# Two-layer decoder trunk on one core: the order of the MLP's loads, products and norms is changed

## The chip, the cores and the metric

The kernel runs on one core of one Trainium2 chip. The metric is the device time of one execution in microseconds (us), lower is better. One core has five engines with a queue each (TensorE = PE, VectorE = DVE, ScalarE = ACT, GpSimd = POOL, SyncE = SP); all DMAs of this kernel that matter here are issued by SP, in the order of its queue.

## The reference, cut to what matters

A trunk of one layer A (stick-breaking attention) and one layer B (differential attention), width 1024, 1024 tokens and 16 meta tokens, each layer with the same MLP (hidden width 4096):

```python
def rmsnorm(x, g):
    y = xf * lax.rsqrt(jnp.mean(xf * xf, axis=-1, keepdims=True) + EPS)
    return y * g
def squared_relu_mlp(x, g, w_in, w_out):
    h = rmsnorm(x, g)
    return jnp.square(jax.nn.relu(h @ w_in)) @ w_out
...
x = x + attention(...); x = x + squared_relu_mlp(x, ...)   # A, then B
```

## The kernel before, in words

Every float32 factor is held as a high and a low part (`acopy` casts the high part on ACT, `tt` subtracts to the low part on DVE); a product is three matmuls (high·high, high·low, low·high). `mlp_stage` (line 736) does one layer's MLP, with names ending in `a` for layer A and in `b` for layer B. Both matrix products of the MLP are done by a seven-product scheme for 2x2 blocks: sums and differences of blocks are formed on DVE, and seven block products take the place of eight. The order of instructions on each engine is made by a scheduler that may move an instruction ahead of others which it doesn't depend on; `pin` and `keep_in_program_order` hold an instruction at its place in the program.

- **Transition** (`step`, L768 on). The attention's output projection is summed into `opa` (one tile for 128 output features and one chunk of tokens, 24 matmuls) and added to the residual `hs`; squares are gathered in `acca`. After tile 3 of the next chunk `rms_of` sums the squares by `rsa` matmuls, after tile 4 `normed` spreads the factor by `rba` transposes and DVE scales `h` (L117). Before these steps `w_split` prepares the seven weight operands of unit 0 (`w1a` to `w7a`).
- **Units** (`unit`, L919). There are 16 units, each making 256 hidden features by seven products `mia`. Unit 0 runs in two parts, for the two halves of the tokens; its product order is `PROD0` = 1, 2, 5, 3, 6, 7, 4 (L732), that of the others `PROD1` = 1, 5, 6, 2, 7, 3, 4. During unit 0's first part the norm of the second half is made (`second`, L1009), and the seven operands of that half (`ops7`: `xca`, `y3a`, `y6a`, `y7a`, `xda`) are cast and subtracted. At its end each unit stores seven results to DRAM (`u_d`, L979).
- **Out-products** (loop L1083). The seven products of `PROD2` = 2, 1, 6, 7, 4, 5, 3 follow, each of 16 steps `fi`. A step loads `ba` (L1091, from `u_d`) and in products 2 and 3, for every second step, `a12a` (L1095): this is the streamed part. Other weights stay resident: `r11a` (four loads), `ra0a`, `ra1a` (three each) and `ra2a` (two), 1 MB each, L1062, and the residual `hqa` (L1058, eight loads of 0.5 MB). The table `loads` (L1063) places them among the steps, but nothing pins them. `wba`, `waa` are the split operands in eight buffers, `moa` the sums in PSUM (24 matmuls of 260 columns a step in A; `mob`, 12 of 512 columns in B).
- **End of the stage.** After the last product (3) `half_add` adds all of `moa` to `hqa`, `row` in `epilogue_a` casts to the next stage's input `xb` and gathers squares in `accx`, and `norms` sums them (`rsx`). Layer B starts with the weights of head 0: `bws` (L1308, three loads each) scaled on POOL (L1314), split into `bwh`, `bwl`, used by `bpj`; `xm`, the meta tokens, is copied on POOL by `pcopy` (L124). In B the stage ends with stores to the output (L1570).

Of the kernel before, what the change touches and what calls it, by code (L numbers as in the profile page):

```python
# [17 lines left out]
P = 128  # L18
# [60 lines left out]
def kernel(ctx: ExitStack, tc: tile.TileContext, inp, out):  # L79
# [652 lines left out]
    PROD0, PROD1 = (1, 2, 5, 3, 6, 7, 4), (1, 5, 6, 2, 7, 3, 4)  # L732
# [3 lines left out]
    def mlp_stage(li, WO, wo_src, wo_scale, O, views, kf, gcol, base, close_w, chunk_done, epilogue):  # L736
# [122 lines left out]
        def ops7(c):  # L859

            h = hs[c]
            B11, B12, B21, B22 = (h[:, 4 * kh:4 * kh + 4, nh * nn:nh * nn + nn] for kh in range(2) for nh in range(2))

            return [lambda: put(c, 1, B11), lambda: put(c, 2, B21), lambda: tt(B11, B12, B11, ALU.subtract),
                    lambda: put(c, 5, B11), lambda: put(c, 3, B22), lambda: tt(B12, B22, B12, ALU.subtract),
                    lambda: tt(B22, B22, B11, ALU.subtract), lambda: put(c, 6, B22), lambda: put(c, 7, B12),
                    lambda: tt(B21, B21, B22, ALU.subtract), lambda: put(c, 4, B21)]
# [51 lines left out]
        def unit(u, parts, prods, more):  # L919
# [6 lines left out]
            for pi, cs in enumerate(parts):  # L926
# [12 lines left out]
                for pn, i in enumerate(prods):  # L939
# [49 lines left out]
        for i in PROD1:  # L989
            w_split(0, i)  # L990

        for ci, v in enumerate(order):
            for m in range(NMF, KT):
                step(m, v, 0)
                if ci and m == NMF:
                    chunk_done(hs, order[ci - 1], ps1, srow)
                    r = rms_of(order[ci - 1])
                if ci and m == NMF + 1:
                    normed(order[ci - 1], r)
                    if ci == 2:  # L1000
# [11 lines left out]
        def second(pi, pn):  # L1012
# [6 lines left out]
            elif pn == 2:  # L1019
# [3 lines left out]
                X7[0] = {1: xc[:, 0], 2: xc[:, 1], 5: xc[:, 2]} | {i: xblk(f"y{i}{tag}") for i in (3, 6, 7)}  # L1023
# [5 lines left out]
        unit(0, ((1,), (0,)), PROD0, second)  # L1029
        st_h0.close()  # L1030
        for u in range(1, NPAIR):
            unit(u, ((0, 1),), PROD1, lambda *a: None)
# [16 lines left out]
        def load_q(mh, nh):  # L1049

            for h in range(2):
                if li:
                    o = 512 * h + 256 * nh
                    nc.sync.dma_start(out=H[:, 4 * h + 2 * nh:4 * h + 2 * nh + 2, 512 * mh:512 * mh + 512],
                                      in_=y_d[o:o + 256, 512 * mh:512 * mh + 512].rearrange("(b q) n -> q b n", q=P))
# [8 lines left out]
        loads = {2: {1: [lambda: load_w(-1, 0)], 4: [lambda: load_w(-1, 4)], 7: [lambda: load_w(-1, 8)],  # L1064
                     9: [lambda: load_q(0, 0)], 11: [lambda: load_w(-1, 12)], 14: [lambda: load_w(0, 0), lambda: load_w(1, 0)]},
# [4 lines left out]
        def half_add(mh, nh, pss):  # L1070

            for x, ps in enumerate(pss):
                if li:
                    hv = H[:, 4 * (x // 2) + 2 * nh + x % 2, 512 * mh:512 * mh + 512]
                else:
                    m, h = divmod(x, 2)
                    hv = H[:, 4 * mh + m, half * h + nn * nh:half * h + nn * nh + nn]
                tt(hv, hv, ps, ALU.add)

        pss = None  # L1080
        for i in PROD2:
            if i in (2, 1, 5):
                qs = [ps2(f"mo{tag}_{i}_{x}") for x in range(2 if li else 4)]  # L1083
                pss = [q[:, x, :512 if li else nn] for q in qs for x in range(2)]
            a12 = None
            for fi in range(NPAIR):
                for fn in loads.get(i, {}).get(fi, ()):
                    fn()
                a11, a21, a22 = r11[:, fi], res(0, fi)[:, 0], res(1, fi)[:, 0]
                bs = srow(f"b{tag}_{i}_{fi}")[:, :half]  # L1090
                nc.sync.dma_start(out=bs, in_=u_d[:, fi, i - 1, :half])  # L1091
                if i in (2, 3):
                    if fi % 2 == 0:
                        a12 = raw(f"a12{tag}_{i}_{fi}").rearrange("p a b -> p (a b)").rearrange("p (f n) -> p f n", n=512)
                        nc.sync.dma_start(out=a12, in_=wr[1, :, fi:fi + 2, :512])  # L1095
                    a = a12[:, fi % 2]
                    if i == 3:
                        tt(a, a, a11, ALU.subtract)
                elif i == 7:
                    a = srow(f"a{tag}_{i}_{fi}")[:, :512]  # L1100
                    tt(a, a22, a11, ALU.subtract)
                else:
                    if i == 6:
                        tt(a21, a21, a22, ALU.add)
                        tt(a11, a21, a11, ALU.subtract)
                    a = {1: a11, 6: a11, 4: a22, 5: a21}[i]
                w, b = wop(f"wa{tag}_{i}_{fi}"), wop(f"wb{tag}_{i}_{fi}")
                for t, s, n in ((w, a, 512), (b, bs, half)):
                    acopy(t[:, 0, :n], s)
                    tt(t[:, 1, :n], s, f(t[:, 0, :n]), ALU.subtract)  # L1110
                first, last = fi == 0 and i in (2, 1, 5), fi == NPAIR - 1
                for x, ps in enumerate(pss):
                    for wi, (p, q) in enumerate(((0, 0), (0, 1), (1, 0))):
                        if li:
                            mm(ps, b[:, p, x * P:x * P + P], w[:, q, :512], first and wi == 0, last and wi == 2, skip_group_check=True)
                        else:
                            m, h = divmod(x, 2)
                            mm(ps, w[:, p, m * P:m * P + P], b[:, q, h * nn:h * nn + nn], first and wi == 0, last and wi == 2,
                               skip_group_check=True)
                work(3)  # L1120
            mh, nh = {2: (0, 0), 1: (0, 0), 6: (0, 1), 7: (1, 1), 4: (1, 0), 5: (1, 1), 3: (0, 1)}[i]
            half_add(mh, nh, pss)
# [34 lines left out]

    def epilogue_a(i, mh, nh, H, mw, hq, ps1):

        if i in (1, 4):  # L1160
            return []
        accx = acc_["x"] = acc_["x"] if acc_ else hq.tile([P, T], F32, name="accx")
        for c in range(3 if i == 5 else 0):
            XB.append(act_tile(c, "xb"))

        def row(m, c, a, n):
            t0 = CH[c][0] + a
            hv = H[:, m, t0:t0 + n]
            acopy(XB[c][:, 0, m, a:a + n], hv)
            tt(XB[c][:, 1, m, a:a + n], hv, f(XB[c][:, 0, m, a:a + n]), ALU.subtract)  # L1170
            acc = accx[:, t0:t0 + n]
            if t0 not in accd:
                act(acc, hv, AF.Square)
                accd.add(t0)
            else:
                sq = mw.tile([P, 520], F32, tag="s", bufs=5, name=f"sqx{t0}_{m}")[:, :n]
                act(sq, hv, AF.Square)
# [424 lines left out]
```

## Time and profile before

| | |
|---|---|
| median of 3 runs | 2783.24 us (2782.41 to 2785.28) |
| profiled execution | 2783.41 us, its span 2781.6 us, mean granted TensorE clock 0.975 |
| PE busy | 2635.3 us of the span (95%) |
| DVE, ACT, POOL busy | 1997.8, 1515.7, 327.1 us |
| moved by DMA | 341.80 MB, mean 123 GB/s |

The profile's times are from the span's start. By its lines, layer A's transition ends at about 740 us, its units run to about 1081 us and its out-products to 1421.8 us; layer B's transition ends at about 2112 us, its units at about 2446 us, its out-products at 2777.1 us. An engine row ends with the idle time before it and what ended that time.

### The profile page before, as it was taken

How to read it: one execution, taken by the hardware profiler on the slowest of the kernel's cores; microseconds unless marked ns; L12 is line 12 of the kernel's file. 1: busy time of each engine (PE TensorE's matmuls, PEld its weight loads, DVE VectorE, ACT ScalarE, POOL GpSimd, SP SyncE). 2: the span in 40 equal slices, each digit the busy share in tenths (PEclk: the TensorE clock that was granted, in tenths of full speed). 3: DMA queues.
4: the chain of work that ended last, by engine and by line, in shares of the span. 5: the costliest groups of instructions: out<-in, count | busy, mean ns of one | idle time of the engine just before them, and what ended most of it. 6: DMA issues, size and time to landing. Idle time of an engine off the chain costs nothing. (4 is left out here: it accounts for less than half of the span.)

```text
span 2781.6 us, 50340 instructions
## 1 busy us (share of the span) xinstructions
PE 2635.3 (95%) x18367; PEld 2495.0 (90%) x18367; DVE 1997.8 (72%) x4007; ACT 1515.7 (54%) x3544; POOL 327.1 (12%) x807
## 2 busy tenths in 40 slices
PE   7999999989899998999989999999998999989999
PEld 7889899878899998999989889989898999967787
DVE  6899999887866565665767888888777666557655
ACT  4666666664355553344546666766544555534443
POOL 2211111000000000000034334443100000000000
PEclk9999999999899999999999999999999999989999
DMA  7333233346144348633431112112452343594333
GB/s 204 100 83 81 74 82 83 106 139 182 50 138 159 136 162 297 210 101 102 134 87 43 39 55 54 54 54 82 139 175 87 134 160 133 176 378 118 93 110 121
DMA packets 298714, 341.80 MB, mean 123 GB/s; under 512 B 32537, under 2 KB 209346, under 8 KB 298466
## 3 DMA queue, kind: packets, MB, share of 16 engines
q1 hardware_dynamic: 289106, 334.32, 39.0%
q10 hardware_dynamic: 9360, 4.26, 0.6%
q8 instruction: 145, 2.38, 0.4%
q14 instruction: 103, 0.84, 0.1%
HBM read 206.99 MB, written 97.28 MB: 109 GB/s over the span
## 5 line engine op out<-in xcount | busy, mean ns | idle before, releaser
L159 PE MATMUL moa<-wba,waa 128*128 128x260 f32 x2688 | 329.4, 286 | 14.2 <-ACT wba L99 14.2
L159 PEld LDWEIGHTS moa<-wba,waa 128*128 128x128 f32 x2688 | 328.2, 191 | 15.0 <-ACT wba L99 14.8
L159 PE MATMUL mob<-wab,wbb 128*128 128x512 f32 x1344 | 319.8, 400 | 12.9 <-ACT wbb L99 10.7
L159 PEld LDWEIGHTS mob<-wab,wbb 128*128 128x128 f32 x1344 | 256.6, 192 | 75.1 <-ACT wbb L99 12.0
L159 PE MATMUL pj<-xa,wh 128*128 128x400 f32 (+2 forms) x1152 | 294.9, 335 | 8.8 <-DVE rsa L667 6.6
L159 PE MATMUL bpj<-bwh,xb 128*128 128x384 f32 x1024 | 285.0, 347 | 4.8 <-ACT k L99 3.4
L159 PEld LDWEIGHTS pj<-xa,wh 128*128 128x128 f32 x1152 | 205.2, 195 | 10.6 <-POOL ws L121 6.8
L159 PEld LDWEIGHTS bpj<-bwh,xb 128*128 128x128 f32 x1024 | 188.8, 191 | 9.4 <-ACT k L99 5.7
L497 DVE TENSOR_TENSOR_SCAN kp<-kp 128x144 f32<-128x144 f32 (+7 forms) x128 | 185.4, 1453 | 11.7 <-ACT kp L105 11.0
L159 PE MATMUL pj<-xa,wl 128*128 128x384 f32 (+2 forms) x576 | 192.8, 335 | 0.0
L159 PE MATMUL bpj<-bwl,xb 128*128 128x384 f32 x512 | 175.2, 342 | 0.0
L1314 POOL TENSOR_SCALAR bws<-bws,gains 128x128 f32<-128x128 f32 (+1 forms) x128 | 65.2, 514 | 837.7 <-DMA bws<-in_b_w_q_dram 772.9
L105 ACT ACTIVATE w<-sc,rsa 128x392 f32<-128x392 f32 (+4 forms) x224 | 121.4, 543 | 33.1 <-PE sc L159 31.6
L105 ACT ACTIVATE kp<-sc,rsa 128x392 f32<-128x392 f32 (+4 forms) x224 | 120.1, 538 | 13.3 <-DVE w L113 13.2
L1373 DVE TENSOR_REDUCE mxb<-sc_b 128x1 f32<-128x144 f32 (+6 forms) x224 | 109.2, 503 | 21.0 <-PE sc_b L159 19.7
L113 DVE TENSOR_TENSOR wt<-pt,wt 128x512 fp32r<-128x512 f32 x160 | 106.4, 681 | 23.0 <-ACT wt L99 22.3
L99 ACT CAST wt<-pt 128x512 fp32r<-128x512 f32 x160 | 90.2, 586 | 56.3 <-PE av L159 51.2
L159 PE MATMUL av<-wt,v 128*128 128x256 f32 x640 | 108.9, 293 | 6.7 <-DVE wt L113 4.4
L159 PEld LDWEIGHTS pj<-xa,wl 128*128 128x128 f32 x576 | 111.8, 194 | 0.5
L162 PE MATMUL pt<-cst,w 128*128 128x128 f32 x640 | 104.8, 278 | 5.9 <-DVE w L113 2.7
L113 DVE TENSOR_TENSOR w<-w,kp 128x143 f32<-128x143 f32 (+7 forms) x128 | 108.4, 852 | 2.0
L159 PEld LDWEIGHTS av<-wt,v 128*128 128x128 f32 x640 | 90.6, 192 | 10.6 <-DVE wt L113 6.5
(486 smaller groups left out, 7448.7 us busy)
## 6 DMA issues: line engine op xcount, KB each, us to landing
ba<-u_d SPq DMA_DIRECT2D x112, 260.0 KB, 2.7
bb<-u_d SPq DMA_DIRECT2D x112, 256.0 KB, 2.7
mwsa<-in_mlp_w_in_dram SPq DMA_DIRECT2D x32, 512.0 KB, 3.9
mwsb<-in_mlp_w_in_dram SPq DMA_DIRECT2D x32, 512.0 KB, 3.8
o_d<-oh SPq DMA_DIRECT2D x52, 256.0 KB, 2.5
ws<-in_a_w_qkv_dram SPq DMA_DIRECT2D x24, 512.0 KB, 4.5
qb<-q SPq DMA_DIRECT2D x128, 64.0 KB, 2.0
a12a<-in_mlp_w_out_dram SPq DMA_DIRECT2D x16, 512.0 KB, 3.6
```

The lines of the kernel that those rows point to most:

```text
L99: nc.scalar.copy(out=o, in_=i)
L105: nc.scalar.activation(out=o, in_=i, func=func, **kw)
L113: nc.vector.tensor_tensor(out=o, in0=a, in1=b, op=op)
L159: return nc.tensor.matmul(o, lhsT=l, rhs=r, start=start, stop=stop, **kw)
L162: return nc.tensor.transpose(out=o, in_=i, identity=ident)
L497: nc.vector.tensor_tensor_scan(out=rv, data0=rv, data1=rv, initial=1.0, op0=ALU.mult, op1=ALU.bypass)
L1314: nc.gpsimd.tensor_scalar(out=ws[:, s], in0=ws[:, s], scalar1=gains[:, gc + k:gc + k + 1], scalar2=1.0, op0=ALU.mult, op1=ALU.mult)
L1373: nc.vector.tensor_reduce(out=mx[:, j:j + 1], in_=ps[:, 0], axis=AX.X, op=ALU.max, negate=True)
```

## The change

1. The loads of resident weights and of the residual are pinned, and their places in product 2 are later.
2. Unit 0 uses `PROD1` as well; `ops7` makes operand 5 ahead of 2 and 3.
3. In the transition `rms_of` and `normed` come one tile later, and unit 0's weight splits are spread over the second chunk's steps.
4. Of the last product, the last four steps are held: for each PSUM half (`x`) the four steps' matmuls are issued together, then the add, and then (`bank_done`) the casts and squares of that half in A, or its output store in B.
5. `xm` is copied on ACT.

```diff
-    PROD0, PROD1 = (1, 2, 5, 3, 6, 7, 4), (1, 5, 6, 2, 7, 3, 4)
+    PROD1 = (1, 5, 6, 2, 7, 3, 4)
...
-            return [lambda: put(c, 1, B11), lambda: put(c, 2, B21), lambda: tt(B11, B12, B11, ALU.subtract),
-                    lambda: put(c, 5, B11), lambda: put(c, 3, B22), lambda: tt(B12, B22, B12, ALU.subtract),
+            return [lambda: put(c, 1, B11), lambda: tt(B11, B12, B11, ALU.subtract), lambda: put(c, 5, B11),
+                    lambda: tt(B12, B22, B12, ALU.subtract), lambda: put(c, 3, B22), lambda: tt(B22, B22, B11, ALU.subtract),
...
-                if ci and m == NMF:
+                if ci and m == NMF + 1:
                     chunk_done(hs, order[ci - 1], ps1, srow)
                     r = rms_of(order[ci - 1])
-                if ci and m == NMF + 1:
+                if ci and m == NMF + 2:
                     normed(order[ci - 1], r)
...
+                if ci == 1:
+                    for i in splits[:2 if m > NMF + 2 else 1]:
+                        w_split(0, splits.pop(0))
...
-                    nc.sync.dma_start(out=H[:, 4 * mh:4 * mh + 4, s], in_=h_d[:, 4 * mh:4 * mh + 4, s])
+                    pin(nc.sync.dma_start(out=H[:, 4 * mh:4 * mh + 4, s], in_=h_d[:, 4 * mh:4 * mh + 4, s]))
...
-            nc.sync.dma_start(out=t, in_=wr[max(k, 0), :, f0:f0 + 4, c0:c0 + 512])
-
-        loads = {2: {1: [lambda: load_w(-1, 0)], 4: [lambda: load_w(-1, 4)], 7: [lambda: load_w(-1, 8)],
...
+            pin(nc.sync.dma_start(out=t, in_=wr[max(k, 0), :, f0:f0 + 4, c0:c0 + 512]))
+
+        loads = {2: {4: [lambda: load_w(-1, 0)], 6: [lambda: load_w(-1, 4)], 8: [lambda: load_q(0, 0)],
...
+            held = 4 if i == PROD2[-1] else 0
+            for fi in range(NPAIR - held):
...
+                w, b = operands(i, fi)
+                for x in range(nb):
+                    products(i, fi, x, w, b)
...
+            if held:
+                work(len(todo))
+                ops = [(fi, *operands(i, fi)) for fi in range(NPAIR - held, NPAIR)]
+            for x in range(nb):
+                if held:
+                    for fi, w, b in ops:
+                        products(i, fi, x, w, b)
+                half_add(mh, nh, x)
+                if held:
+                    bank_done(x, mh, nh, H, mw)
...
-        pcopy(xm[:, :, 0:NM], f(XB[0][:, 0, :, 0:NM]))
-        pcopy(xm[:, :, 32:48], f(XB[0][:, 1, :, 0:NM]))
+        acopy(xm[:, :, 0:NM], f(XB[0][:, 0, :, 0:NM]))
+        acopy(xm[:, :, 32:48], f(XB[0][:, 1, :, 0:NM]))
```

**Where instructions move, SP at layer A's first out-product.** SP's queue where unit 15's stores (`u_d`) and product 2's loads stand; the number in `ba_6` is the step. Before:

```order
L1091 DMA ba_6_13276<-u_d 128x520
L1062 DMA ra0a<-in_mlp_w_out_dram 128x4x512
L1062 DMA ra1a<-in_mlp_w_out_dram 128x4x512 x2
L1062 DMA ra0a<-in_mlp_w_out_dram 128x4x512
L1062 DMA ra1a<-in_mlp_w_out_dram 128x4x512
L979 DMA u_d<-u1a_12853 128x520
L1062 DMA ra0a<-in_mlp_w_out_dram 128x4x512
L1091 DMA ba_7_13311<-u_d 128x520
```

The same queue with the change, from the row ahead of `ba_8` on:

```order
L979 DMA u_d<-u4a_12857 128x520
L1084 DMA ba_8_13344<-u_d 128x520
L1084 DMA ba_9_13378<-u_d 128x520
L1088 DMA a12a_12_13480<-in_mlp_w_out_dram 128x2x512
L1084 DMA ba_10_13411<-u_d 128x520
L1064 DMA r11a<-in_mlp_w_out_dram 128x4x512 x3
L1084 DMA ba_11_13445<-u_d 128x520
L1064 DMA r11a<-in_mlp_w_out_dram 128x4x512
L1088 DMA a12a_14_13548<-in_mlp_w_out_dram 128x2x512
L1084 DMA ba_12_13478<-u_d 128x520
L1084 DMA ba_13_13512<-u_d 128x520
L1064 DMA ra1a<-in_mlp_w_out_dram 128x4x512
```

Between `ba_6` and `ba_11` there stand two `hqa` and three `r11a` loads, where before there stood all eight `ra` and all eight `hqa` loads; `ra0a`, `ra1a` and `ra2a` now come from behind `ba_13` of product 2 to behind `ba_10` of product 1. Layer B's queue is changed in the same way.

**PE at layer A's transition and unit 0.** The rows before (`opa_4` is tile 4 of the last-but-one chunk; `mia_0` is the first part of unit 0):

```order
L159 MATMUL rsa_8889<-ones,acca_8480 128x2 x3
L159 MATMUL opa_4_8896<-oa_7586,woa_8499 128x256 x24
L162 MATMUL rba_8926<-cst,ra_8890 128x128 x3
...
L159 MATMUL mia_0_2_9243<-xba,w3a_8678 128x260 x12
L159 MATMUL mia_0_0_9241<-xba,w6a_8665 128x260 x12
L159 MATMUL mia_0_0_9241<-x7a,w7a_8673 128x260 x12
L159 MATMUL mia_0_0_9241<-x4a,w4a_8681 128x260 x12
L159 MATMUL mia_1_0_9397<-xca,w1a_8656 128x260 x12
```

With the change:

```order
L159 MATMUL opa_4_8864<-oa_7586,woa_8499 128x256 x24
L159 MATMUL rsa_8894<-ones,acca_8480 128x2 x3
L159 MATMUL opa_5_8905<-oa_7586,woa_8508 128x256 x24
L162 MATMUL rba_8935<-cst,ra_8895 128x128 x3
...
L159 MATMUL mia_0_0_9241<-x7a,w7a_8995 128x260 x12
L159 MATMUL mia_0_2_9243<-xba,w3a_9030 128x260 x12
L159 MATMUL mia_0_0_9241<-x4a,w4a_9033 128x260 x12
L159 MATMUL mia_1_0_9397<-xca,w1a_8861 128x260 x12
L159 MATMUL mia_1_1_9398<-xca,w5a_8902 128x260 x12
L159 MATMUL mia_1_0_9397<-y6a,w6a_8957 128x260 x12
```

`rsa` and `rba` stand one tile later, 12 matmuls stand between product 7 and product 4, which share one PSUM tile, and `y6a` is wanted ahead of `xca`'s operand for product 2.

**SP at the end of layer A's stage.** Before:

```order
L1091 DMA ba_15_16973<-u_d 128x520
L1308 DMA bws_0_17198<-in_b_w_q_dram 128x128
L1308 DMA bws_0_17198<-in_kv_w_dram 128x128 x2
L1308 DMA bws_1_17208<-in_b_w_q_dram 128x128
L1181 DMA h_d<-hqa 128x4x260 x2
```

With the change:

```order
L1084 DMA ba_15_16901<-u_d 128x520
L1194 DMA h_d<-hqa 128x4x260
L1331 DMA bws_0_17198<-in_b_w_q_dram 128x128
L1331 DMA bws_0_17198<-in_kv_w_dram 128x128 x2
L1194 DMA h_d<-hqa 128x4x260
L1331 DMA bws_1_17208<-in_b_w_q_dram 128x128
```

The first weights of layer B now stand behind a store of the finished residual.

## Rows read from the trace of the kernel before

**Rows 1.** The page: busy time of each engine, share of the span, instructions.

```profile
PE 2635.3 (95%) x18367; PEld 2495.0 (90%) x18367; DVE 1997.8 (72%) x4007; ACT 1515.7 (54%) x3544; POOL 327.1 (12%) x807
```

**Rows 2.** Stages: window, its length, busy time (instructions) by engine, clock, DMA.

```profile
core 0: us, PE busy (x) PEld busy (x) DVE busy (x) ACT busy (x) POOL busy (x), PEclk, DMA share, GB/s
745.00:782.00 37.00, 29.31 (x205) 27.88 (x206) 29.55 (x47) 20.11 (x39) 0.00 (x0) 0.86 0.22 74
1068.00:1140.00 72.00, 57.83 (x438) 57.02 (x437) 36.31 (x58) 24.31 (x42) 0.00 (x0) 0.88 1.01 370
1140.00:1420.00 280.00, 280.00 (x2330) 280.00 (x2329) 182.28 (x344) 125.58 (x252) 0.85 (x2) 1.00 0.39 108
1420.00:1450.00 30.00, 20.21 (x110) 19.14 (x109) 21.21 (x87) 18.08 (x65) 16.67 (x40) 0.77 0.41 114
1450.00:2030.00 580.00, 555.29 (x3706) 522.41 (x3704) 460.38 (x1507) 381.15 (x1275) 208.59 (x630) 0.99 0.23 65
2435.00:2505.00 70.00, 59.29 (x268) 48.65 (x267) 36.64 (x60) 24.35 (x43) 0.00 (x0) 0.88 1.02 378
2505.00:2770.00 265.00, 262.79 (x1133) 212.23 (x1132) 161.92 (x257) 106.68 (x187) 0.00 (x0) 1.00 0.39 110
```

**Rows 3.** PE in time order, product 2 of layer A: start, us, and idle time before.

```profile
1111.00 5.00 PE L159 MATMUL moa<-wba,waa 128*128 128x260 f32 x24 [9.17 <-ACT wba L99]
1116.86 12.05 PE L159 MATMUL moa<-wba,waa 128*128 128x260 f32 x96 [0.87 <-ACT wba L99]
1133.05 7.16 PE L159 MATMUL moa<-wba,waa 128*128 128x260 f32 x35 [4.13 <-ACT wba L99]
```

**Rows 4.** PE in time order, product 2 of layer B.

```profile
2472.36 7.97 PE L159 MATMUL mob<-wab,wbb 128*128 128x512 f32 x24 [5.23 <-ACT wbb L99]
2482.43 12.97 PE L159 MATMUL mob<-wab,wbb 128*128 128x512 f32 x48 [2.09 <-ACT wbb L99]
2498.78 6.54 PE L159 MATMUL mob<-wab,wbb 128*128 128x512 f32 x16 [3.39 <-ACT wbb L99]
```

**Rows 5.** SP's queue in time order, product 2 of layer A.

```profile
1079.17 2.39 SPq L1091 DMA_DIRECT2D ba<-u_d  x1
...
1102.62 0.32 SPq L1091 DMA_DIRECT2D ba<-u_d  x1
...
1114.02 5.78 SPq L1062 DMA_DIRECT2D r11a<-in_mlp_w_out_dram  x4
```

**Rows 6.** DMA issues (KB each, median us to landing), 1068 to 1140.

```profile
ba<-u_d SPq DMA_DIRECT2D x16, 260.0 KB, 7.9
```

**Rows 7.** PE in time order, layer A's transition and unit 0.

```profile
702.55 1.42 PE L159 MATMUL rsa<-ones,acca 128*128 128x2 f32 x6 [5.85 <-DVE acca L113]
703.83 5.39 PE L159 MATMUL opa<-oa,woa 128*128 128x256 f32 x24
...
759.42 2.97 PE L159 MATMUL mia<-x4a,w4a 128*128 128x260 f32 x12 [4.73 <-ACT u3a L99]
```

**Rows 8.** DVE in time order, unit 0 of layer A.

```profile
749.02 4.42 DVE L117 SCALAR_TENSOR_TENSOR h0a<-h0a,gains,rba 128x400 f32<-128x400 f32 x8 [2.38 <-PE rba L162]
...
764.60 1.24 DVE L113 TENSOR_TENSOR y6a<-h0a,y6a 128x1040 fp32r<-128x1040 f32 x1
```

**Rows 9.** PE in time order, unit 0 of layer B.

```profile
2130.01 2.93 PE L159 MATMUL mib<-x4b,w4b 128*128 128x256 f32 x12 [4.89 <-ACT u3b L99]
```

**Rows 10.** PE, POOL and SP in time order, the handover to layer B.

```profile
1427.83 3.39 PE L159 MATMUL rsx<-ones,accx 128*128 128x2 f32 x16 [5.97 <-DVE accx L113]
1434.49 0.45 PE L159 MATMUL bpj<-bwh,xm 128*48 128x256 f32 x1 [3.27 <-POOL xm L124]
...
1434.91 1.97 POOL L1314 TENSOR_SCALAR bws<-bws,gains 128x256 f32<-128x256 f32 x4
...
1413.11 0.33 SPq L1308 DMA_DIRECT2D bws<-in_b_w_q_dram  x1
```

**Rows 11.** DVE in time order, the last adds of layer B.

```profile
2775.74 2.68 DVE L113 TENSOR_TENSOR hqb<-hqb,mob 128x512 f32<-128x512 f32 x4 [7.76 <-PE mob L159]
```

More of the change, by code (lines that the diff above doesn't have):

```diff
@@ L988, in mlp_stage @@
         w_load(1)
-        for i in PROD1:
-            w_split(0, i)
+        splits = list(PROD1)
         for ci, v in enumerate(order):
@@ L1027, in second @@
                 work(3)
-        unit(0, ((1,), (0,)), PROD0, second)
+        unit(0, ((1,), (0,)), second)
         st_h0.close()
         for u in range(1, NPAIR):
-            unit(u, ((0, 1),), PROD1, lambda *a: None)
+            unit(u, ((0, 1),), lambda *a: None)
         st_x.close()
@@ L1073, in half_add, with products @@
+        def products(i, fi, x, w, b):
+            first, last = fi == 0 and i in (2, 1, 5), fi == NPAIR - 1
+            for wi, (p, q) in enumerate(((0, 0), (0, 1), (1, 0))):
                 if li:
-                    hv = H[:, 4 * (x // 2) + 2 * nh + x % 2, 512 * mh:512 * mh + 512]
+                    l, r = b[:, p, x * P:x * P + P], w[:, q, :512]
                 else:
                     m, h = divmod(x, 2)
-                    hv = H[:, 4 * mh + m, half * h + nn * nh:half * h + nn * nh + nn]
@@ L1087, in mlp_stage @@
                 for fn in loads.get(i, {}).get(fi, ()):
                     fn()
[L1089 to L1119, printed above, removed]
@@ L1156, in norms, with row_a @@
             nc.vector.tensor_copy(out=rsx[:p, q], in_=y)
-    def epilogue_a(i, mh, nh, H, mw, hq, ps1):
[L1160 to L1177, printed above, removed]
-                tt(acc, acc, sq, ALU.add)
+    def row_a(H, mw, m, c, a, n):
+        t0 = CH[c][0] + a
+        hv = H[:, m, t0:t0 + n]
+        acopy(XB[c][:, 0, m, a:a + n], hv)
+        tt(XB[c][:, 1, m, a:a + n], hv, f(XB[c][:, 0, m, a:a + n]), ALU.subtract)
+        acc = acc_["x"][:, t0:t0 + n]
+        if t0 not in accd:
+            act(acc, hv, AF.Square)
+            accd.add(t0)
+        else:
+            sq = mw.tile([P, 520], F32, tag="s", bufs=5, name=f"sqx{t0}_{m}")[:, :n]
+            act(sq, hv, AF.Square)
+            tt(acc, acc, sq, ALU.add)
+    def epilogue_a(i, mh, nh, H, mw, hq, ps1):
         def store(mh, t0):
             nc.sync.dma_start(out=h_d[:, 4 * mh:4 * mh + 4, t0:t0 + 260], in_=H[:, 4 * mh:4 * mh + 4, t0:t0 + 260])
+        if i == 3:
+            return [lambda c=c: norms(ps1, c) for c in range(3)] + [lambda h=h: store(0, 520 * h + 260) for h in range(2)]
+        if i != 5:
+            return []
+        acc_["x"] = hq.tile([P, T], F32, name="accx")
+        for c in range(3):
+            XB.append(act_tile(c, "xb"))
         out_ = []
-        for mh, nh in [(0, 0), (1, 0), (1, 1)] if i == 5 else [(0, 1)]:
+        for mh, nh in ((0, 0), (1, 0), (1, 1)):
             for h in range(2):
```

86 lines of the change are left out of this document (58 added, 28 removed).

## The prediction

> **What bounds the kernel now.** I read the page's busy times first, then the table of stages, then PE's rows in time order wherever a stage showed PE less than full, and last the queue or engine that ended each wait. PE is busy 2635.3 of 2781.6 us [rows 1], so what can be won without taking away matmuls is at most the 146 us in which it idles, and the time in which its clock is low. The stages [rows 2] say where: in 1140:1420 PE is busy all 280.00 us at a granted clock of 1.00, so 2330 matmuls of 260 columns set the pace there, 280.00/2330 = 0.1202 us each, 24 of them 2.88 us. In 2505:2770 the pace of the 512-column matmuls is 262.79/1133 = 0.232 us, 12 of them 2.78 us. Four kinds of stretch are worse: the first out-product of each layer (1068:1140 and 2435:2505, clock 0.88, DMA busy 1.01 and 1.02 of its engines at 370 and 378 GB/s), the transition with unit 0 (655:745, 745:782 at 0.86), and the handover (1420:1450, clock 0.77). These are the stretches that the change touches. Layer B's attention (1450:2030) idles only 580 - 555.29 = 24.7 us.
>
> In product 2 of layer A PE waits three times for the split of a streamed `ba` (ACT `wba`): 9.17, 0.87 and 4.13 us [rows 3]. ACT is not slow: SP issued two `ba` following each other at 1079.17 and 1102.62 [rows 5], 23 us apart, since resident loads stood between them; a `ba` took 7.9 us to land [rows 6], and 1102.62 + 7.9 = 1110.5 is just ahead of PE's restart at 1111.00. Layer B shows the same with 5.23, 2.09 and 3.39 us [rows 4].
>
> The profiled execution took 2783.41 us and the median is 2783.24; I count from 2783.4, and the two agree. From no change a measurement of this kernel can tell about 0.2%, 5.6 us.
>
> **The change part by part.**
>
> *Loads, layer A.* No transfer is added or removed; sixteen loads (eight `ra`, eight `hqa`, 12.6 MB at 1.05 and 0.53 MB each) left their place ahead of `ba_11`, and two `hqa` and three `r11a` (4.2 MB) stand there instead. What the stage loses now: 72 us hold 438 matmuls [rows 2], which at full pace take 438 x 0.1202 = 52.6 us; 19.4 us are lost, 14.17 of them the waits, the other 5.2 a half-speed clock after the waits (24 matmuls took 5.00 us where 2.88 would do, 35 took 7.16 where 4.21 would [rows 3]). Do the waits go? Steps 0 to 7 are done at 1111.00 - 9.17 = 1101.83, so without waits step 11 begins at 1101.83 + 3 x 2.88 = 1110.5 and step 15 at 1122.0. From `ba_7` to `ba_11` the new queue moves five `ba` and six `u_d` (0.27 MB each), two `a12a` (0.52), two `hqa` and three `r11a`: 8.2 MB, at 0.370 MB/us 22 us. Even if `ba_7` goes out no earlier than before (1079.17), `ba_11` lands at 1101, 9 us early. To `ba_15` it is 13.5 MB, 36.5 us, 1115.7, 6 us early. The 8.4 MB of `ra` and most `hqa` go into products 1 and 6, where DMA is busy 0.39. So I take the whole: **-19.4**. Bounds: -20, and -12.5, where the last wait with its clock stays (4.13 + 2.95).
>
> *Loads, layer B.* Waits 10.71 us; clock 7.97 - 24 x 0.232, 12.97 - 48 x 0.232 and 6.54 - 16 x 0.232, together 7.0 [rows 4], less 0.16 a row for the pipelined end of the last matmul: 17.2. A step is 2.78 us here, so the slack is 0.1 us a step less. **-17.2**, bounds -18 and -11.
>
> *Norms a tile later, layer A.* `rsa` waits 5.85 us for DVE's `acca` [rows 7]. Now 24 matmuls of `opa_4` go first; 256 columns at about 0.12 us are 2.9 us of work in the wait. Its end stays, since the weight splits ahead of `acca` on DVE keep their order. **-2.9**; -6 if the half clock of the 5.39 us row goes too, 0 if `acca` slips as far.
>
> *Product order of unit 0.* Before product 4, PE waits 4.73 us for ACT's `u3a` copy of product 7 [rows 7]: both products use one PSUM tile. Twelve matmuls (1.44 us) now stand between. But `y6a`, which DVE finished at 764.60 + 1.24 = 765.8 [rows 8], is now wanted third in the second part, and everything there hangs on 4.42 us of scaling by DVE [rows 8], which is busy 29.55 of the 37 us [rows 2]. PE's wait moves to DVE: **0**, bounds -4 and +1. Layer B has the same wait, 4.89 us [rows 9], and the same successor, and there the splits of unit 0 really move later on DVE: **0**, bounds -3 and +2.
>
> *The last product by banks, with `xm` on ACT.* PE waits 5.97 us for `accx` and 3.27 us for `xm` [rows 10]. Half of the adds and row work is now under the second half's matmuls, and the copies pass from POOL, where memsets and weight scalings stood ahead, to ACT. Against that, all eight operand buffers are held to the end: the load of `bws_0`, issued at 1413.11 [rows 10], now waits for their release about the end of the last product (1421.8), 8.7 us later, and `bws_1` stands behind a residual store. 9.24 us of waits against 8.7 us of later start, with four scalings taking 1.97 us on POOL [rows 10] for each following pair of weight tiles: **-1**, bounds -5 and +2. In layer B the add of the last bank ends the work; of four adds in 2.68 us [rows 11] three come earlier, but PE pauses for operands between the banks: **0**, bounds -1 and +1.
>
> *Layer B's attention.* The moved copies shift some casts between ACT and DVE there, and the scheduler orders that stage anew. PE idles 24.7 us in it: a fifth of that either way, **0**, bounds -5 and +5.
>
> Sum: -19.4 - 17.2 - 2.9 - 1 = -40.5, 2783.4 - 40.5 = **2743 us**.
>
> **The rivals.**
>
> *The stall moves down the queue (2756 us).* In the trace the third wait, 4.13 us [rows 3], came after four `r11a` were issued from 1114.02 [rows 5] with the next `ba` behind them. In the new order three of them still stand ahead of `ba_11`, and now pinned there. If the lead that I counted (9 us) is not built up, because buffers and not the queue hold the stream back, the third wait and its slow clock stay in both layers: 4.13 + 2.95 + 3.39 + 2.83 = 13.3 us, 2756. For it: DMA runs at its shown full rate to the end of the stage. Against: in the trace the 22 us of lead were eaten by sixteen loads, not three. The Trainium skill, page "DMA: Bandwidth & Descriptors", section "Queues, rings and completion order", says that each DMA engine takes descriptors in ring order and that SP has one row of rings for all its DMAs; by that rule a streamed load can't overtake a resident one whatever its urgency, which would make this rival's 2756 of the sum wherever lead is missing, and leave 2743 where it is not. The trace agrees: `ba` takes 7.9 us there.
>
> *Only the loads pay (2752 us).* DVE becomes the bound in both units 0 and the later weight chain outweighs the shorter tail: 36.6 us won, and the upper bounds of the other terms (+1, +2, +2) given back: 2783.4 - 36.6 + 5 = 2752. For it: DVE is the busiest engine in 745:782. Against: two waits on PE there lie plainly ahead of other ready work.
>
> *The collision is only put off (2780 us).* If the deferred 8.4 MB starve product 1 as they did product 2, the gain is nil. Against: the stage at 0.39 DMA share has room for them.
>
> *Slower (2797 us).* Pinning makes SP stop at the first `r11a` till the units' last reads and stores are done, with `ba_11` and everything after queued behind. Without lead, PE starves from 1110.5 on. A `ba` needs 7.9 us to land, so SP must be free by about 1101, and each us beyond costs one in each layer; slower than before takes over 46 us, a release after 1124; at 1128, 2 x 27 us: 2783.4 - 40.5 + 54 = 2797. For it: before, `r11a` went out only at 1114.02. Against: what it waits for are stores that stood in the same jam, and that now go first.
>
> **How the numbers follow.** Forecast 0.60, stall moves 0.16, only the loads 0.14, put off 0.06, slower 0.04. So faster 0.90, same 0.06, slower 0.04. The range goes down to 2729 (the lower bounds of transition and handover, and half of the others) and up to 2763, which holds the two rivals with some of their own spread; outside lie about 2 in 10.
>
> **What would show it.** In the changed profile: PE at clock 1.00 and without a wait over 1 us in product 2 of both layers, `ba` landing in under 8 us ahead of need, the `ra` loads in product 1 at no cost to PE; `rsa`'s wait near 3 us; the waits for `u3a` and `u3b` gone and new ones on DVE in their place; `rsx` waiting some 2 us and the first `bpj` about as late as before after the last `moa`. I'm wrong if `ba_11` or `ba_12` ends a PE wait of over 3 us, if SP stands at `r11a`, or if layer B's attention changes by over 5 us.

## The result, and the profile after

The changed kernel takes **2751.86 us** (median of 4 runs, 2750.98 to 2753.60) against 2782.82 us beside it: ratio 0.9891, 95% interval 0.9873 to 0.9908. That is 31 us faster; the forecast was 2743 us, 40 us faster, with a range of 2729 to 2763. The sign and the range held, the gain fell short by 9 us.

The page shows where the waits of product 2 went. Line, engine, operation and tile; count; busy time and mean ns; idle time before the group and who ended most of it:

```profile
L159 PE MATMUL moa<-wba,waa 128*128 128x260 f32 x2688 | 325.3, 284 | 0.4 <-DVE wba L113 0.4
...
L159 PE MATMUL mob<-wab,wbb 128*128 128x512 f32 x1344 | 313.8, 394 | 3.4 <-DVE hqb L113 2.8
```

Of the 3.4 us of `mob`, 2.8 are for `hqb`, behind finished products. In product 2 of layer B PE has this one wait, in time order (start, us, instruction, idle time before):

```profile
2481.31 38.60 PE L159 MATMUL mob<-wab,wbb 128*128 128x512 f32 x164 [0.56 <-DVE wbb L113]
```

The 14.17 us of layer A [rows 3] are 0.4 us now, the 10.71 us of layer B [rows 4] 0.56 us. The stages of the changed kernel (window, length, busy time and instructions by engine, clock, DMA share, GB/s; to be held against [rows 2]):

```profile
1073.00:1140.00 67.00, 66.56 (x552) 66.35 (x551) 42.95 (x72) 29.82 (x51) 0.00 (x0) 1.00 0.93 339
1140.00:1390.00 250.00, 250.00 (x2074) 250.00 (x2073) 169.98 (x320) 116.64 (x237) 0.00 (x0) 1.00 0.47 134
...
2420.00:2490.00 70.00, 69.44 (x340) 57.71 (x339) 46.31 (x75) 31.72 (x55) 0.00 (x0) 1.00 0.93 339
```

The DMA engines are still busy 0.93 of product 2, but PE runs through at clock 1.00. The second window is for product 1 and later, which took over the deferred loads: DMA 0.47, PE without idle.

Unit 0 of layer A is the stretch that got worse. From the last `opa` to its end, about the same matmuls, before and with the change:

```profile
740.50:776.20 35.70, 26.73 (x183) 25.09 (x181) 31.05 (x48) 19.77 (x37) 0.00 (x0) 0.86 0.11 35
739.60:779.40 39.80, 28.74 (x182) 26.83 (x181) 33.80 (x49) 20.24 (x38) 0.00 (x0) 0.79 0.08 25
```

Of the 4.1 us more, 2.1 are idle time of PE (9.0 before, 11.1 now) and 2.0 longer busy time for the same work, at a granted clock of 0.79 instead of 0.86.

SP's queue in product 2 of layer A, in time order, and the landing times there:

```profile
1078.49 0.32 SPq L1084 DMA_DIRECT2D ba<-u_d  x1
...
1092.25 1.48 SPq L1064 DMA_DIRECT2D r11a<-in_mlp_w_out_dram  x3
1093.78 1.64 SPq L1084 DMA_DIRECT2D ba<-u_d  x1
```

```profile
ba<-u_d SPq DMA_DIRECT2D x13, 260.0 KB, 10.8
```

`ba_11`, behind three `r11a`, goes out at 1093.78; with the median of 10.8 us it lands near 1104.6 (an estimate). A `ba` now takes longer to land than before (7.9 us, [rows 6]), and that costs nothing: PE wants it near 1113.7, the 1110.5 of the prediction and 3.2 us by which this execution came later to the first `moa`.

The sum by stretches. Each runs from the first or last PE instruction of one tile to that of another; "transition" is from the first `opa` (`opb`) to the end of unit 0, "handover" from the last `moa` to the 64th `bpj`. The two attention stretches are the parts that the change was not meant to touch:

| stretch (us) | before | after | moved | forecast |
|---|---|---|---|---|
| attention A, start to first `opa` | 659.3 | 662.7 | +3.4 | 0 |
| transition and unit 0, A | 117.1 | 116.9 | -0.2 | -2.9 |
| first `moa` to last | 351.7 | 333.9 | -17.8 | -19.4 |
| handover | 26.0 | 25.8 | -0.2 | -1 |
| attention B, to first `opb` | 587.2 | 584.3 | -2.8 | 0 |
| transition and unit 0, B | 111.9 | 114.3 | +2.3 | 0 |
| first `mob` to last | 340.9 | 325.4 | -15.5 | -17.2 |
| last `mob` to the end | 4.5 | 3.8 | -0.7 | 0 |

The two spans differ by 31.4 us, and these rows give it (the other units moved by 0.04 us at most). So the two product-2 stretches brought -33.3 of the -36.6 that was forecast for them, and the rest, forecast at -3.9, brought +1.2 outside attention.

Where unit 0 of layer A now waits, PE in time order (start, us, instruction, idle time before and what ended it):

```profile
705.91 0.80 PE L159 MATMUL rsa<-ones,acca 128*128 128x2 f32 x6 [3.51 <-DVE acca L113]
...
746.26 1.59 PE L159 MATMUL rsa<-ones,acca 128*128 128x2 f32 x8 [3.57 <-DVE acca L113]
...
756.55 1.71 PE L159 MATMUL mia<-xba,w3a 128*128 128x260 f32 x12 [1.71 <-DVE u1a L113]
...
764.12 1.70 PE L159 MATMUL mia<-xca,w5a 128*128 128x260 f32 x11 [2.31 <-DVE xca L113]
767.65 0.58 PE L159 MATMUL mia<-y6a,w6a 128*128 128x260 f32 x1 [1.82 <-ACT y6a L99]
769.54 2.75 PE L159 MATMUL mia<-y6a,w6a 128*128 128x260 f32 x11 [1.31 <-DVE y6a L113]
```

The first `rsa` waits 3.51 us instead of 5.85 [rows 7], as forecast; but the last one waits 3.57 us. In the kernel before its row was this:

```profile
744.88 0.96 PE L159 MATMUL rsa<-ones,acca 128*128 128x2 f32 x8 [1.28 <-DVE acca L113]
```

So 2.3 us more are lost there. The 4.73 us ahead of product 4 [rows 7] are gone. In their place stand 1.71 us for `u1a`, a finished sum that DVE takes from PSUM, and 2.31 + 1.82 + 1.31 = 5.44 us for operands of the second half (the high part is cast on ACT, the low part comes from DVE). The kernel before had a wait for `u1a` too, and three of 0.46 us:

```profile
768.87 1.70 PE L159 MATMUL mia<-y3a,w3a 128*128 128x260 f32 x12 [1.57 <-DVE u1a L113]
```

Without the last `rsa`, PE's waits in this unit add up to 7.7 us before and 7.5 now: the new product order exchanged one wait for others, and the last `rsa` is what the unit lost. Layer B:

```profile
2099.70 2.65 PE L159 MATMUL mib<-xbb,w6b 128*128 128x256 f32 x12 [3.12 <-ACT u1b L99]
...
2107.80 1.69 PE L159 MATMUL mib<-xbb,w3b 128*128 128x256 f32 x12 [1.72 <-DVE u1b L113]
...
2115.27 1.58 PE L159 MATMUL mib<-xcb,w5b 128*128 128x256 f32 x11 [2.27 <-DVE xcb L113]
2118.76 0.58 PE L159 MATMUL mib<-y6b,w6b 128*128 128x256 f32 x1 [1.91 <-ACT y6b L99]
2121.83 2.72 PE L159 MATMUL mib<-y6b,w6b 128*128 128x256 f32 x11 [2.49 <-DVE y6b L113]
```

Here 4.89 us [rows 9] were exchanged for the last four, 8.4 us, and ahead of them stand 3.12 us for `u1b`, where the kernel before waited 1.69 us for the norm (`rbb`). The handover, PE and then SP:

```profile
1408.94 2.12 PE L159 MATMUL rsx<-ones,accx 128*128 128x2 f32 x16 [1.68 <-DVE accx L113]
1415.57 0.42 PE L159 MATMUL bpj<-bwh,xm 128*48 128x256 f32 x1 [4.51 <-DVE nx L117]
...
1423.30 0.32 PE L159 MATMUL bpj<-bwh,xm 128*48 128x256 f32 x1 [1.38 <-ACT bwh L99]
```

```profile
1406.14 0.33 SPq L1331 DMA_DIRECT2D bws<-in_b_w_q_dram  x1
```

`rsx` waits 1.68 us instead of 5.97 [rows 10], and the first `bpj` comes 8.4 us after the last `moa` instead of 12.7. But PE then waits for the split weights (`bwh`), and the 64th `bpj` comes only 0.2 us sooner (table). `bws_0` is loaded 1.0 us ahead of the last `moa`'s end (1407.14), where it was 8.6 us ahead before.

### The profile page after: what moved, and what is told of

Same layout as the page of the kernel before. It is cut to its first block, busy times and chain, and to the rows that moved or that the text cites. A ratio compares the mean times of both kernels' runs of the same rounds, so it can differ in the third digit from the quotient of the medians.

```text
span 2750.2 us, 50318 instructions
## 1 busy us (share of the span) xinstructions
PE 2629.2 (96%) x18367; PEld 2486.8 (90%) x18367; DVE 1997.4 (73%) x4009; ACT 1516.4 (55%) x3544; POOL 332.4 (12%) x805
## 4 chain that ended last, share of the span: by engine, by line
PE 66%; DVE 11%; ACT 3%; DMA 3%; issue 2%; POOL 1%; SPq 0%; DVEq 0%; ACTq 0%; POOLq 0%
PE mia L159 11%; PE mib L159 11%; PE moa L159 11%; PE mob L159 9%; PE bpj L159 8%; PE opb L159 2%; DVE kp L497 2%; PE sc_b L159 2%; PE avb L159 2%; PE pj L159 2%; PE opa L159 1%; DVE wt L113 1%; PE ofb L159 1%; DMA bb<-u_d 1%; DVE w L113 1%
## 5 line engine op out<-in xcount | busy, mean ns | idle before, releaser
L159 PE MATMUL mob<-wab,wbb 128*128 128x512 f32 x1344 | 313.8, 394 | 3.4 <-DVE hqb L113 2.8
L105 ACT ACTIVATE kp<-sc,rsa 128x392 f32<-128x392 f32 (+4 forms) x224 | 120.3, 539 | 12.8 <-DVE w L113 12.7
```

Of the source, the lines that this page charges most:

```text
L105: nc.scalar.activation(out=o, in_=i, func=func, **kw)
L159: return nc.tensor.matmul(o, lhsT=l, rhs=r, start=start, stop=stop, **kw)
```

## The experiments

All times in us; the stretches are those of each kernel's profiled execution, whose whole time can lie some us off the median (old norms 2750.28, two orders 2731.44). No pins, hybrid order and more VectorE work were run once, the others four or five times. "The same" in the last two rows is two orders with old norms.

| kernel | median | attention A | transition A | `moa` | handover | attention B | transition B | `mob` |
|---|---|---|---|---|---|---|---|---|
| the change | 2751.86 | 662.7 | 116.9 | 333.9 | 25.8 | 584.3 | 114.3 | 325.4 |
| old order | 2740.94 | 663.8 | 115.7 | 332.6 | 25.6 | 582.8 | 109.0 | 325.4 |
| old norms | 2745.46 | 666.5 | 117.2 | 333.9 | 25.6 | 581.6 | 111.4 | 325.4 |
| no banks | 2744.45 | 661.4 | 115.8 | 334.0 | 26.9 | 581.9 | 113.0 | 324.6 |
| only the loads | 2746.11 | 663.7 | 116.9 | 332.6 | 26.2 | 583.1 | 109.7 | 324.2 |
| no pins | 2773.73 | 657.9 | 116.9 | 350.5 | 26.1 | 580.4 | 111.7 | 341.7 |
| hybrid order | 2746.73 | 663.7 | 117.8 | 334.2 | 25.7 | 579.4 | 111.3 | 325.7 |
| two orders | 2741.72 | 654.9 | 116.7 | 332.6 | 25.9 | 577.0 | 109.9 | 325.8 |
| two orders, old norms | 2736.18 | 659.8 | 117.0 | 332.6 | 25.4 | 582.5 | 106.8 | 325.5 |
| the same, more VectorE work | 2743.90 | 664.2 | 117.9 | 332.6 | 25.1 | 577.9 | 112.2 | 325.4 |
| the same, GpSimd differences | 2749.27 | 660.8 | 120.2 | 332.6 | 25.0 | 581.4 | 114.2 | 326.5 |

A warning stands in the column of attention A. In all these rows and in the kernel before, PE, DVE, ACT and POOL execute the same instructions in the same order up to the first `opa`, and yet it comes anywhere from 654.9 to 666.5 us. The experiments were run on three chips, but on one of them alone (no pins to two orders, old norms) it is 654.9 to 663.7. Runs of one kernel differ as much (old order: 2730.92 to 2743.51 us). So these kernels are told apart by their stretches rather than by their medians. Transition A agrees within 1.1 us where its instructions are the same (the change, no banks, no pins: 116.9, 115.8, 116.9). Transition B has a wider spread: with the change's edits there it is 114.3, 113.0 and 111.7 us, with the old ones 111.9 and 109.7 (before, only the loads). Part of that is the scheduler, which with the same edits puts weight splits of unit 1 (`w6b`, `s3b`) once ahead of and once behind `y6b` on DVE: PE's last wait for `y6b` is 2.49 us in the change and 1.28 in no banks.

**Only the loads**, on the kernel before:

```diff
-            nc.sync.dma_start(out=t, in_=wr[max(k, 0), :, f0:f0 + 4, c0:c0 + 512])
+            pin(nc.sync.dma_start(out=t, in_=wr[max(k, 0), :, f0:f0 + 4, c0:c0 + 512]))
...
+        loads = {2: {4: [lambda: load_w(-1, 0)], 6: [lambda: load_w(-1, 4)], 8: [lambda: load_q(0, 0)],
```

> The kernel before with nothing but the pinned loads at their new places. Theory: the waits of product 2 go in both layers with the slow clock behind them; from the first moa to the last 332.5 to 334 us instead of 351.7, from the first mob to the last 324 to 326 us instead of 340.9, and about 2783 - 34 = 2748 to 2750 us, below the whole change at 2752. Rival, part of the gain in product 2 comes from the other edits (the last product by banks, other work on VectorE): waits over 1 us stay in product 2 and the time is above 2755 us.

2746.11 us, ratio 0.9865 (0.9849 to 0.9881). `moa` takes 332.6 us, 19.1 less than before, and `mob` 324.2, 16.7 less: 35.8 us where the forecast had 36.6. The theory holds. All that the change adds to the loads is worth nothing or less: from the first `opa` to the end without attention B the change takes 6 us longer than this kernel, 4.6 of them in transition B.

**No pins**, the new places alone:

```diff
-            pin(nc.sync.dma_start(out=t, in_=wr[max(k, 0), :, f0:f0 + 4, c0:c0 + 512]))
+            nc.sync.dma_start(out=t, in_=wr[max(k, 0), :, f0:f0 + 4, c0:c0 + 512])
```

> The changed kernel with the pins taken off the resident loads, their new places in the program kept. Theory, the pins do it and the places alone nothing: the scheduler puts the loads back ahead of ba_7 to ba_13, PE waits about 14 us in product 2 of layer A and 11 us in layer B again, and from the first moa to the last it is about 352 us (333.9 with the change), from the first mob about 341 (325.4): some 33 us slower than the change. Rival, the later places are enough: waits under 2 us, no slower than the change.

SP's queue in product 2 is the old one again, and so are the waits. PE in product 2 of layer A of this kernel:

```profile
1108.54 4.71 PE L159 MATMUL moa<-wba,waa 128*128 128x260 f32 x24 [8.11 <-ACT wba L99]
1114.47 12.07 PE L159 MATMUL moa<-wba,waa 128*128 128x260 f32 x96 [1.22 <-ACT wba L99]
1130.60 19.58 PE L159 MATMUL moa<-wba,waa 128*128 128x260 f32 x141 [4.07 <-ACT wba L99]
```

`moa` grows by 16.5 us and `mob` by 16.3 over the change, 33 us as the theory had it; the one run, 2773.73 us, shows 22 of them, since attention was 4.8 and 3.9 us shorter in it and transition B 2.6. So the new places win nothing without the pins: the scheduler undoes the table. Pins at the old places were not run, so what they would win alone is not shown.

**Old order** of unit 0's products and operands, the rest as changed:

```diff
-                for pn, i in enumerate(PROD1):
+                for pn, i in enumerate(PROD1 if u else PROD0):
```

> The changed kernel with unit 0 back in its old product order 1, 2, 5, 3, 6, 7, 4 and its operands made in the old order; loads, norms and banks as changed. From the last opa matmul to the end of unit 0 the trace shows 35.7 us before and 39.8 us with the change in layer A (opb: 38.1 and 41.7 us in layer B). Theory, the order costs it (operand 5 and 6 of the second half come late from VectorE): both stretches fall back, to about 36 and 38 us, and the time to about 2744 us. Rival, the norms a tile later cost it (more VectorE work ahead of the norm's squares): they stay near 40 and 42 us, and the time at 2752 us.

2740.94 us, ratio 0.9832 (0.9808 to 0.9856), its interval apart from the change's. From the last `opa` (`opb`) to the end of unit 0 it takes 38.0 us in A and 37.9 in B, where 36 and 38 were expected: as the theory had it in B, where the whole transition falls by 5.3 us, below anything that the change's edits gave there; only half the way in A. There the rival shows in the same trace:

```profile
707.53 0.80 PE L159 MATMUL rsa<-ones,acca 128*128 128x2 f32 x6 [2.29 <-DVE acca L113]
727.47 0.50 PE L159 MATMUL rsa<-ones,acca 128*128 128x2 f32 x4
747.91 0.96 PE L159 MATMUL rsa<-ones,acca 128*128 128x2 f32 x8 [3.58 <-DVE acca L113]
```

The last `rsa` waits 3.58 us with the old order too.

**Old norms**, with the new order; unit 0's weight splits and the work on its first operands go back with them:

```diff
-                if ci and m == NMF + 1:
+                if ci and m == NMF:
...
-                if ci and m == NMF + 2:
+                if ci and m == NMF + 1:
...
-        splits = list(PROD1)
+        for i in PROD1:
+            w_split(0, i)
```

> The changed kernel with the norms and the weight splits of unit 0 back at their old places; order, loads and banks as changed. Theory, the order alone costs unit 0: the stretch from the last opa matmul to the end of unit 0 stays near 39.8 us in layer A and 41.7 us in layer B, while the transition of layer A (from the first opa matmul, 77.1 us with the change) goes back to 81.4 us: about 2756 us. Rival, the later norms cost unit 0: the stretches fall to 36 and 38 us as the transition grows, and the time stays at about 2750 us.

PE in time order here:

```profile
709.70 1.41 PE L159 MATMUL rsa<-ones,acca 128*128 128x2 f32 x6 [6.55 <-DVE acca L113]
728.83 0.50 PE L159 MATMUL rsa<-ones,acca 128*128 128x2 f32 x4
751.37 0.96 PE L159 MATMUL rsa<-ones,acca 128*128 128x2 f32 x8 [1.29 <-DVE acca L113]
```

With norms at their old places the waits are 6.55 and 1.29 us; with the later norms 3.51 and 3.57, or 2.29 and 3.58. From the last `opa` (`opb`) to the end of unit 0 it takes 36.5 and 38.4 us and the `opa` stretch 80.7: the rival holds. That settles the norms in layer A: a tile later moves some 2 to 4 us of waiting from the first norm to the last, whose `acca` now stands behind the later scaling and operand work on DVE (2.3 us more there in every kernel with later norms), and the transition with unit 0 stays at 117 us (117.2 here, 116.9 with the change). In B unit 0 takes 39.5 to 41.7 us with both edits (no banks, no pins, the change), and either edit undone brings it to 38. The 3.1 us for `u1b` stand in those three kernels alone, so that wait takes both edits.

**No banks**, the last product not held:

```diff
-            held = 4 if i == PROD2[-1] else 0
+            last_i, held = i == PROD2[-1], 0
...
+            if last_i:
+                for x in range(nb):
+                    bank_done(x, mh, nh, H, mw)
```

> The changed kernel whose last product isn't held: all steps over all banks, then all adds, then the casts and squares (xm stays on ScalarE). From the last moa matmul to the 64th bpj matmul it was 25.9 us before and 25.8 us with the change. Theory, the banks win about 4 us at the norm and give them back as the first weights of layer B come later: the first bpj later by about 4 us after the last moa, but the 64th no later, time within 2 us of the change (2750 to 2754 us). Rival, the banks are worth their 4 us and something else gave them back: 2756 us.

PE at the handover of this kernel:

```profile
1412.04 3.38 PE L159 MATMUL rsx<-ones,accx 128*128 128x2 f32 x16 [7.12 <-DVE accx L113]
1418.79 0.42 PE L159 MATMUL bpj<-bwh,xm 128*48 128x256 f32 x1 [3.38 <-DVE nx L1169]
```

The first `bpj` comes 14.0 us after the last `moa` instead of 8.4, the 64th 1.1 us later. So the theory holds by the stretches (the median is 7 us lower than the change's, below the expected 2750 to 2754, with attention 3.8 us shorter): 5.6 us won at the first `bpj` are given back but for 1.1. That the weights set the 64th `bpj`, and not the norm, is seen in three other kernels with banks (old order, hybrid order, two orders with old norms): there the first `bpj` comes 5.4 us after the last `moa`, and the 64th at 25.4 to 25.7 us all the same, with waits for `bwl` and `bwh` between. The first `bpj` with the old order:

```profile
1411.12 0.42 PE L159 MATMUL bpj<-bwh,xm 128*48 128x256 f32 x1 [0.77 <-DVE nx L117]
```

In layer B `mob` is 0.8 us shorter without banks and the end 0.7 longer: nothing.

**Hybrid order** 1, 2, 5, 6, 7, 3, 4 in both parts of unit 0, and **two orders**, that one in the first part and the old one in the second, alone and with the **old norms**. The operands are made in the old order in all three. The cut is that of two orders:

```diff
-                for pn, i in enumerate(PROD1):
+                for pn, i in enumerate(PROD1 if u else PROD0[pi]):
```

> The changed kernel with order 1, 2, 5, 6, 7, 3, 4 in both parts of unit 0, operands made in the old order. Theory: in the first part all operands are ready, product 3 hides the copy of product 7, and the 4.8 us wait ahead of product 4 goes; in the second part product 6 comes before 3, so PE waits again for VectorE's y6, 2 to 4 us. From the last opa to the end of unit 0 about 37 us in layer A (39.8 with the change, 38.0 in the old order). Rival, the order doesn't matter and VectorE's norm chain sets the end of unit 0 alone: 38 us or more, as in the old order.

> The changed kernel with order 1, 2, 5, 6, 7, 3, 4 in the first part of unit 0 and the old 1, 2, 5, 3, 6, 7, 4 in the second. Theory, each part has its own limit (the copy of product 7 in the first, VectorE's operand 6 in the second): the 4.8 us wait goes and the second part starts some 5 us earlier, PE then waiting about 2 us for y6; from the last opa to the end of unit 0 33.5 to 35 us in layer A and 33 to 36 in layer B (38.0 and 37.9 in the old order), 2733 to 2738 us. Rival, the 4.8 us only move to the second part, since VectorE sets its end: 38 us again, and 2741 us as in the old order.

> As the kernel with an order for each part of unit 0, and the norms and weight splits at their old places. Theory, the later norms win as much in the transition of layer A (first to last opa matmul 77 us instead of 81) as they lose at the norm in unit 0 (PE waits 3.6 us for the squares instead of 1.3): from the first opa to the end of unit 0 within 1.5 us of the kernel with the later norms. Rival, they win outright: 3 us or more slower here.

The 4.8 us ahead of product 4 go in all three, but from the last `opa` to the end of unit 0 it is 39.7 us in A with the hybrid order and 38.2 with two orders, not the 37 and the 33.5 to 35 that were expected, and transition A doesn't move: 117.8, 116.7, 117.0 us. PE waits again for operands of the second half, as the rivals of the first two said; here with two orders, then with old norms as well:

```profile
764.38 1.58 PE L159 MATMUL mia<-y6a,w6a 128*128 128x260 f32 x11 [2.71 <-DVE y6a L113]
```

```profile
763.84 2.75 PE L159 MATMUL mia<-xca,w5a 128*128 128x260 f32 x11 [3.59 <-DVE xca L113]
```

For the old norms the theory holds in A (117.0 against 116.7 us with the later ones) and its rival, 3 us slower, falls. In layer B two orders give 109.9 us and with old norms 106.8, the shortest of all; the difference of 3 us between them is in the size of the spread there. With old norms the whole takes 2736.18 us, ratio 0.9829 (0.9807 to 0.9850); with the later ones 2741.72, 0.9850 (0.9829 to 0.9872). Both beat the kernel before, and by the stretches from the first `opa` on without attention B they beat the change by 5 and 9 us. Against only the loads that is 1 us longer and 3 us shorter, within the spread of transition B: beyond the loads nothing clear was won.

**More VectorE work**: three passes that change nothing, right ahead of the second half's operands. **GpSimd differences**: four differences moved off DVE. Both on two orders with old norms:

```diff
+                for _ in range(3):
+                    tt(hs[0][:, 0:4, :nn], hs[0][:, 0:4, :nn], hs[0][:, 0:4, :nn], ALU.max)
```

```diff
+            sub = ptt if c == 0 else tt
```

> The kernel with an order for each part of unit 0 and the norms at their old places, with three more passes of 1.24 us on VectorE over the scaled half (a maximum of a block with itself) right ahead of the second half's operands, in each layer. Across the variants so far the stretch from the first opa matmul to the end of unit 0 in layer A has stayed at 115.7 to 117.8 us whatever was reordered, 117.0 in this kernel without the passes. Theory, VectorE's work is what sets the end of unit 0: the stretch grows by nearly all of the 3.7 us, to about 120.5 us, and layer B's likewise from 106.8 to about 110. Rival, the waits of PE belong to the order and VectorE has slack: it grows by less than 1.5 us.

> The kernel with an order for each part of unit 0 and the norms at their old places, with the four block differences of the second half's operands (1.24 us each on VectorE) done by GpSimd, which is idle there. Theory, VectorE's work sets the end of unit 0: freed of 5 us it ends unit 0 earlier by 2 to 4 us a layer, layer A's stretch 113 to 115 us instead of 117.0, unless GpSimd takes over 2.5 us for one, and the time is 2728 to 2734 us. Rival, GpSimd is slow enough that the operands 5 and 6 come later than from VectorE: the stretch is 118 us or more and nothing is won.

With more VectorE work transition A grew by 0.9 us for 3.7 us of added work, so the theory falls there in its plain form. PE waits earlier, 5.01 us for the first operand, and hardly for the later ones:

```profile
766.18 0.59 PE L159 MATMUL mia<-xca,w1a 128*128 128x260 f32 x1 [5.01 <-ACT xca L99]
```

That DVE's work has no part in the end of unit 0 doesn't follow from it: the scheduler also moved weight splits of unit 1 (`w6a`, `s3a`, `w2a`) from ahead of `y6a` on DVE to behind it, so that part of the added work was made up for. In B the transition grew by 5.4 us, more than was added; the theory holds there, though 106.8 us was the shortest of all, the spread is 2.6 us, and it is one run. GpSimd lost in both layers, 3.2 and 7.4 us, as the rival said. Its rows in layer A, DVE's in the same time, and PE's wait for product 5 of the second half:

```profile
756.33 5.80 POOL L121 TENSOR_TENSOR h0a<-h0a 128x1040 f32<-128x1040 f32 x2 [94.06 <-DVE xca L113]
```

```profile
754.96 1.23 DVE L113 TENSOR_TENSOR xca<-h0a,xca 128x1040 fp32r<-128x1040 f32 x1
...
756.78 3.06 DVE L113 TENSOR_TENSOR xca<-h0a,xca 128x1040 fp32r<-128x1040 f32 x1
759.77 3.46 DVE L113 TENSOR_TENSOR y3a<-h0a,y3a 128x1040 fp32r<-128x1040 f32 x1
```

```profile
770.74 2.75 PE L159 MATMUL mia<-xca,w5a 128*128 128x260 f32 x11 [9.15 <-DVE xca L113]
```

A difference takes GpSimd 2.9 us instead of 1.24, and DVE's own instructions stretch from 1.23 to 3.06 and 3.46 us while it runs.

## Why the prediction was right, and where it was not

- **What bounds the kernel.** Right. The two product-2 stretches held the gain, and the cause was the place of the resident loads in SP's one queue: only the loads give 35.8 us, taking the pins away takes 33 back.
- **Loads, -19.4 and -17.2.** Right in mechanism and nearly in size: -19.1 and -16.7 alone. In the whole change they show as -17.8 and -15.5. The missing 1.3 us in A are a slower pace of all `moa`: 2074 matmuls fit in 250 us where before it is 2330 in 280 [rows 2], which is 2080. The change, old norms, no banks and hybrid order, all with product 6 ahead of 3 in unit 0's second part, take 333.9 us or more, the kernels with 3 ahead of 6 332.6. But that order alone isn't the cause: no pins has it too, and once its load waits are over it runs at the faster pace (the row below); why is open. In B 0.8 of the missing 1.2 us are the banks.

```profile
1145.00:1395.00 250.00, 250.00 (x2082) 250.00 (x2081) 166.84 (x311) 116.77 (x235) 0.00 (x0) 1.00 0.39 112
```

- **The stall moves down the queue (2756).** Did not happen, though three `r11a` do stand ahead of `ba_11`. The lead of 9 us was there: `ba_11` went out at 1093.78. The Trainium skill (page "DMA: Bandwidth & Descriptors", section "Queues, rings and completion order") says that each DMA engine takes the descriptors of a ring in order, and also that a later one may finish its write before an earlier one, so the prediction's "can't overtake" goes further than the page. The longer landing behind three `r11a`, 10.8 us instead of 7.9, agrees with the order of the ring; whether a later load ever finishes first, no run here shows.
- **Norms a tile later, -2.9.** Wrong: -0.2 by the stretch. The step that failed is "24 matmuls of `opa_4` go first", which priced only the first `rsa` and named no one for the work that now comes later on DVE. The `opa` stretch did fall, from 81.4 to 77.1 us, and unit 0 rose from 35.7 to 39.8: the last `rsa` lost 2.3 us, shown with either order, and PE's clock in unit 0 fell from 0.86 to 0.79. The prediction's bound of 0, `acca` slipping as far, is near what came, but for the `acca` of the last chunk.
- **Product order of unit 0, 0 in both layers.** In A right: the 4.73 us came back in waits for the operands of the second half and for `u1a`. In B the sum said 0, bounds -3 and +2, and +2.3 was measured; undoing the order gives 5.3 us there, undoing the norms 2.9, with a spread of 2.6 for the same edits. So it costs something together with the later norms; the wait of 3.1 us for `u1b` needs both, and how the rest is shared isn't settled.
- **Banks and `xm`, -1 and 0.** Right in size: 1.1 us in A, nothing in B. The late load of `bws_0` did eat the shorter tail, but not where the prediction's sign looked for it: the first `bpj` was to be "about as late as before", and came 4.3 us sooner; the time was lost between it and the 64th.
- **Only the loads pay (2752).** This rival, at 0.14, has the time that came, 2751.86 us, and in the main its reason: the loads paid, the rest didn't. Its first half is shown in part (PE waits for DVE's operands in both units 0, which lengthens unit 0 but not transition A), its second is not: the weight chain gave back no more than the tail won. That its figure fits to 0.1 us is luck: it has -36.6 + 5, the stretches have -33.3 and +1.2, and attention the remaining +0.6; the loads alone measured 2746.11.
- **Only put off (2780), slower (2797).** Neither came. The deferred loads cost PE no idle time in product 1 (DMA 0.47, PE busy all 250.00 us), and SP sent the first `r11a` at 1092.25, well ahead of the 1101 by which it had to be free.
- **Attention, 0 with 5 either way.** That term was for layer B, and -2.8 is within it. Layer A's attention moved by +3.4, which the sum has nowhere; the same instructions spread over 11.6 us there from execution to execution, which the range should have named as a cause. The 5.6 us that a measurement was said to tell are too few for these kernels: the runs of old order alone span 12.6 us.

## What to carry to other kernels

When one queue feeds a stream and residents, count what stands between two stream loads and where each resident is first needed; a pin may be needed to keep a scheduler from filling early what can wait. When a step is moved later to cover a wait, follow the engine that it frees to the next instruction that waits for it: here each 2 to 5 us taken from one wait in unit 0 came back at a later one, for operands or sums that DVE makes. Compare kernels by stretches that differ, and take the spread from stretches that don't.

## What was not expected of the hardware

The first 660 us, the same instructions on PE, DVE, ACT and POOL, spread over 11.6 us from execution to execution. The granted clock in 0 to 655 us was 0.99 in the earliest (two orders) and 0.97 in the latest (old norms), but it doesn't order the others: the kernel before had 0.97 too, at 659.3 us. VectorE's 1.23 us instruction took 3.06 and 3.46 us beside a GpSimd one of its kind. The matmuls of layer A's out-products run 0.3% slower in some kernels than in others, at a granted clock of 1.00 in both; the product order of unit 0, 300 us earlier, goes along with it in all kernels but one (no pins).
